# Four single B tiles loaded in two or three parts each, and fifteen one-word loads by SyncE

## The chip, the cores and the metric

One core of one Trainium2 chip. The metric is device microseconds of one execution, as the median of several runs. All runs quoted here are fast.

## The reference

```python
def setup_inputs():
    B, N = 8, 2176
    return {"a": randn(B, N, N) as float32, "b": randn(B, N, N) as float32}

def reference(a, b):
    prod = np.matmul(a, b)
    return np.diagonal(prod, axis1=1, axis2=2).sum(axis=-1)      # 8 numbers
```

The trace of a product needs no product: it is the sum over all i, j of a[i, j] * b[j, i]. The kernel has to read 303 MB and to do one multiply and add for each pair of elements.

## The kernel before

For each of the eight products it loads A in two double tiles (128 partitions x 2 x 4 rows) and one single tile (128 x 1 row), transposes A on TensorE, loads B in tiles of the same kinds, and multiplies and sums on VectorE. GpSimd issues nearly all loads, in one fixed order, and each casts float32 to bfloat16 on its way. The buffers are three deep.

```python
stage = ctx.enter_context(tc.tile_pool(name="stage", bufs=3))
single = ctx.enter_context(tc.tile_pool(name="single", bufs=3))
# ... (cut)
loaded = []

def in_order():
    return tc.issue_after(loaded[-1].ins) if loaded else nullcontext()

def load(src, start, m, count):
    if m == 1:
        t = single.tile([P, 1, N], bf16, tag="single")
    else:
        t = stage.tile([P, DOUBLE * ROWS, N], bf16, tag="stage")
    rows = src[start:start + P * m * count, :].rearrange("(g p r) k -> p g r k", g=count, r=m)
    part = t[:, 0:count * m, :].rearrange("p (g r) k -> p g r k", r=m)
    with in_order():
        issued = nc.gpsimd.dma_start(out=part, in_=rows)
    loaded.append(issued)
    groups = [(start + g * P * m, m, t[:, g * m:(g + 1) * m, :]) for g in range(count)]
    return groups, issued
# ... (cut: transposes of A, evacuation, products)
for start, m, count in ([(*g, 1) for g in b_groups] if last else joined(b_groups)):
    # ... (cut: the last tile of the last product)
    groups, _ = load(b[bi], start, m, count)
    for start, m, b_t in groups:
        # ... (cut: the multiply-and-sum on VectorE)
# ... (cut: sums over the partitions by TensorE)
nc.sync.dma_start(out=out.rearrange("(a b) -> a b", a=1), in_=tiles["result"][:1, :BATCH])
```

SyncE does two things only: the first tile of A, and the eight results at the end.

## Time and profile before

| | before |
|---|---|
| median, runs | 710.44 us (710.42 to 710.47, 2 runs) |
| span of the profiled run | 708.7 us |
| last load landed | 705.28 us |
| output issued, landed | 706.78, 707.87 us |
| packets of GpSimd's queue q0 | 11,472 |
| packets of SyncE's queue q1 | 146 |

How to read it: all times within a run count from the start of its span. A load is cut into packets for sixteen DMA engines. In a single tile a packet is one row, 4,352 bytes as written; in the double tiles it is four rows, 17,408 bytes. "Row" below means one of 4,352 bytes. Each engine finishes its share by itself and then adds one to the load's semaphore, so the trace has sixteen completion times for one load of GpSimd, and the load has landed with the last of them. I call the engine that completes last the latest engine, and the distance from the first completion to the last one the spread. The records name no engine, so the sixteen times are only a sorted list. The lines of the profile that carry the reading stand in the prediction below.

```profile
SPq L342 <- DMA out_dram<-result: 0.4, 1, 0.4
```

### The profile page before, as it was taken

The numbers are of one execution on the slowest core, as the hardware profiler recorded it, in microseconds if no ns is written. First come the engines' busy times: TensorE is split into PE (matmuls) and PEld (weight loads), VectorE is DVE, ScalarE is ACT, GpSimd is POOL, SyncE is SP. The second block draws the span as 40 slices with busy tenths as digits, with TensorE's granted clock in tenths as the row PEclk, the third lists the DMA queues.
The fourth block names the chain that finished last, engine by engine and source line by source line (L and its number), as shares of the span: only waits on it lengthen the run. The fifth ranks groups of instructions, "written<-read, shape, count | busy, mean of one in ns | idle before, by whom it ended". The sixth has DMA issues, their size and how long they took to land.

```text
span 708.7 us, 3573 instructions
## 1 busy us (share of the span) xinstructions
PE 197.8 (28%) x1342; PEld 184.2 (26%) x1342; DVE 420.6 (59%) x455; ACT 196.8 (28%) x210; POOL 35.0 (5%) x61
## 2 busy tenths in 40 slices
PE   1542006420055100551006600056000670006705
PEld 0542005410054100550006500056000560005605
DVE  0223996139952399523994349943499334993396
ACT  2344005430064200652006510066000670006700
POOL 1000000000010000100001000000000000000010
PEclk9977556765577655776557765577655775557765
DMA  9999999999999999999999999999999999999997
GB/s 220 220 220 214 209 221 220 219 210 213 223 219 213 214 218 220 219 211 214 220 220 216 212 216 220 217 214 214 220 220 215 213 217 219 217 216 214 217 215 143
DMA packets 11635, 152.30 MB, mean 215 GB/s; under 512 B 866, under 2 KB 1122, under 8 KB 3298
## 3 DMA queue, kind: packets, MB, share of 16 engines
q0 software_dynamic: 11472, 150.97, 100.1%
q1 hardware_dynamic: 146, 1.11, 0.4%
q8 instruction: 10, 0.16, 0.1%
q14 instruction: 7, 0.06, 0.0%
HBM read 303.04 MB, written 0.00 MB: 428 GB/s over the span
## 4 chain that ended last, share of the span: by engine, by line
DMA 54%; DVE 29%; another core or an unknown queue 10%; PE 3%; issue 2%; ACT 1%; POOL 1%; DVEq 0%; POOLq 0%
DMA t<-in_b_dram 42%; DVE scratch L132 29%; DMA t<-in_a_dram 12%; PE ps L165 2%; ACT at L122 1%; POOL t L83 1%; PE trace_ps L293 0%; DVE acc L132 0%; DVEq L132 0%; PE ps L186 0%; POOL identity masks.py:199 0%; DVE at L120 0%; PE total L308 0%; POOL identity masks.py:197 0%
## 5 line engine op out<-in xcount | busy, mean ns | idle before, releaser
L132 DVE CUSTOM_DVE_ANT_1 scratch<-at,t 128x2048 bf16<-128x2048 bf16 (+1 forms) x159 | 319.6, 2010 | 76.7 <-DMA t<-in_b_dram 69.4
L122 ACT COPY at<-ps 128x1024 bf16<-128x1024 bf16 x208 | 194.5, 1039 | 472.0 <-PE ps L165 472.0
L165 PE MATMUL ps<-identity,t 128*128 128x128 f32 x1071 | 176.8, 332 | 480.5 <-DMA t<-in_a_dram 255.4
L165 PEld LDWEIGHTS ps<-identity,t 128*128 128x128 f32 x1071 | 164.9, 213 | 489.2 <-DVE sums L285 322.0
L120 DVE COPY at<-ps 128x1024 bf16<-128x1024 bf16 (+2 forms) x104 | 93.6, 903 | 201.0 <-PE ps L165 183.7
L83 POOL DMA_DIRECT2D t<-in_a_dram x23 | 15.4, 669 | 357.8 <-DVE acc L132 213.3
L83 POOL DMA_DIRECT2D t<-in_b_dram x27 | 17.0, 632 | 292.8 <-DVE acc L132 145.0
L186 PE MATMUL ps<-identity,t 128*128 128x128 bf16 x170 | 16.4, 219 | 5.3 <-DVE at L120 5.0
L293 PE MATMUL trace_ps<-t,at 128*128 128x128 bf16 x80 | 9.6, 290 | 22.7 <-DMA t<-in_b_dram 22.3
L293 PEld LDWEIGHTS <-at 128*128 128x128 bf16 x89 | 9.8, 122 | 23.6 <-issue 22.9
L186 PEld LDWEIGHTS <-t 128*128 128x128 bf16 x170 | 13.0, 100 | 8.5 <-issue 8.3
L132 DVE DVE_READ_ACCUMULATOR2_ANT acc<- 128x1 f32 x166 | 13.6, 82 | 0.0
L96 DVE CAST t<-words 128x1088 bf16<-128x1088 f32 x1 | 0.7, 727 | 5.0 <-DMA words<-in_a_dram 5.0
L132 DVE CUSTOM_DVE_ANT_1 scratch<-at,b_t 128x256 bf16<-128x256 bf16 (+1 forms) x3 | 1.5, 515 | 1.6 <-DMA b_t<-in_b_dram 1.6
L132 DVE CUSTOM_DVE_ANT_0 scratch<-at,t 128x128 bf16<-128x128 bf16 x7 | 2.0, 291 | 0.2
L95 ACT CAST t<-words 128x1088 bf16<-128x1088 f32 x1 | 1.1, 1098 | 3.8 <-DMA words<-in_a_dram 3.8
L258 POOL DMA_DIRECT2D b_t<-in_b_dram x3 | 1.6, 567 | 0.0
L285 DVE TENSOR_REDUCE sums<-acc 128x1 f32<-128x22 f32 (+1 forms) x8 | 1.4, 174 | 0.3
L95 ACT ACT_TABLE_LOAD x1 | 1.3, 1283 | 0.7 <-PEq L331 0.7
L293 PE MATMUL trace_ps<-b_t,at 128*128 128x128 bf16 x9 | 1.3, 290 | 0.0
L308 PE MATMUL total<-late,ones 128*1 128x1 f32 x8 | 0.5, 163 | 0.3 <-DVE late L132 0.3
masks.py:199 POOL TENSOR_SCALAR_AFFINE_SELECT identity<-identity 128x128 f32<-128x128 f32 (+1 forms) x2 | 0.5, 307 | 0.0
(14 smaller groups left out, 2.4 us busy)
## 6 DMA issues: line engine op xcount, KB each, us to landing
t<-in_a_dram POOLq DMA_DIRECT2D x16, 4352.0 KB, 44.1
t<-in_b_dram POOLq DMA_DIRECT2D x14, 4352.0 KB, 51.8
t<-in_b_dram POOLq DMA_DIRECT2D x3, 2176.0 KB, 32.4
t<-in_b_dram POOLq DMA_DIRECT2D x9, 544.0 KB, 54.8
t<-in_a_dram POOLq DMA_DIRECT2D x7, 544.0 KB, 45.5
words<-in_a_dram SPq DMA_DIRECT2D x1, 1088.0 KB, 5.1
t<-in_b_dram POOLq DMA_DIRECT2D x1, 1088.0 KB, 14.7
b_t<-in_b_dram POOLq DMA_DIRECT2D x1, 256.0 KB, 19.6
```

The lines of the kernel that those rows point to most:

```text
L83: issued = nc.gpsimd.dma_start(out=part, in_=rows)
L95: nc.scalar.copy(out=t[:, 0, :half], in_=plain[:, :half])
L96: nc.vector.tensor_copy(out=t[:, 0, half:], in_=plain[:, half:])
L120: last_copy = nc.vector.tensor_copy(out=dst, in_=src)
L122: nc.scalar.copy(out=dst, in_=src)
L132: nc.vector.tensor_tensor_reduce(out=out, in0=x, in1=y, scale=1.0, scalar=0.0, op0=MUL, op1=ADD, accum_out=acc,)
L165: nc.tensor.transpose(ps[:, n * m + r, :], words[:, r, c0:c0 + step * (P - 1) + 1:step], tiles[f32],)
L186: last_transpose = nc.tensor.transpose(ps16[:, n, r, :], a_t[:, r, c0:c0 + P], tiles[bf16],)
L258: loaded.append(nc.gpsimd.dma_start(out=row[:, lo:hi], in_=b[bi, start:start + P, lo:hi]))
L285: nc.vector.reduce_sum(out=tiles["sums"][:, bi:bi + 1], in_=acc[:, :cols], axis=mybir.AxisListType.X)
L293: nc.tensor.matmul(trace_ps, x, y, start=(n == 0), stop=(n == len(pe_work) - 1),)
L308: nc.tensor.matmul(total[:, BATCH - 1:BATCH], tiles["ones"], part, start=(n == 0), stop=(n == len(parts) - 1),)
```

## The change

The single B tile of products 1 to 4 (the products count from 0) is loaded in parts of unequal partition counts. SyncE also loads single words to 1, 2, ... 15 partitions, once the third load has landed; nothing reads them. The bytes of A and B stay the same. The intent is to see how a load whose partition count is no multiple of sixteen is dealt to the sixteen DMA engines.

```diff
+    SPLIT_SINGLES = {
+        1: ((0, 120), (120, P)),
+        2: ((0, 120), (120, 124), (124, P)),
+        3: ((0, 104), (104, 116), (116, P)),
+        4: ((0, 112), (112, P)),
+    }
+    MARKS = 15
...
+            parts = SPLIT_SINGLES.get(bi, ((0, P),)) if m == 1 else ((0, P),)
...
-        with in_order():
-            issued = nc.gpsimd.dma_start(out=part, in_=rows)
-        loaded.append(issued)
+        for lo, hi in parts:
+            with in_order():
+                if len(parts) == 1:
+                    issued = nc.gpsimd.dma_start(out=part, in_=rows)
+                else:
+                    issued = nc.gpsimd.dma_start(out=part[lo:hi], in_=rows[lo:hi])
+            loaded.append(issued)
...
+        if bi == 0:
+            marks = const.tile([MARKS, MARKS], f32, tag="marks")
+            for n in range(1, MARKS + 1):
+                begun = nc.sync.dma_start(out=marks[0:n, n - 1:n], in_=a[0, 0:n, 0:1])
+                tc.add_manual_dep(begun.ins, loaded[2].ins.name, ...)   # after the third load
```

More of the change, by code (lines that the diff above doesn't have):

```diff
@@ L72, in in_order, with load @@
         return tc.issue_after(loaded[-1].ins) if loaded else nullcontext()
-    def load(src, start, m, count):
+    def load(src, start, m, count, parts=((0, P),)):
         if m == 1:
@@ L270 @@
                 continue
-            groups, _ = load(b[bi], start, m, count)
+            parts = SPLIT_SINGLES.get(bi, ((0, P),)) if m == 1 else ((0, P),)
+            groups, _ = load(b[bi], start, m, count, parts)
             for start, m, b_t in groups:
@@ L283 @@
                     on_dve(at[:, v0:v0 + m, split:], b_t[:, 0:m, split:])
+        if bi == 0:
+            marks = const.tile([MARKS, MARKS], f32, tag="marks")
+            for n in range(1, MARKS + 1):
+                begun = nc.sync.dma_start(out=marks[0:n, n - 1:n], in_=a[0, 0:n, 0:1])
+                tc.add_manual_dep(
+                    begun.ins, loaded[2].ins.name,
+                    mybir.DependencyInfo(
+                        mybir.DependencyClass.Sync, mybir.DependencyReason.DATA
+                    ),
+                    reason="after the third load",
+                )
         nc.vector.reduce_sum(
```

## The prediction

> **What bounds the kernel now.** I read the page first: the busy shares, the slices and the table of DMA queues.
>
> ```profile
> PE 197.8 (28%) x1342; PEld 184.2 (26%) x1342; DVE 420.6 (59%) x455; ACT 196.8 (28%) x210; POOL 35.0 (5%) x61
> ...
> DMA  9999999999999999999999999999999999999997
> ...
> q0 software_dynamic: 11472, 150.97, 100.1%
> q1 hardware_dynamic: 146, 1.11, 0.4%
> q8 instruction: 10, 0.16, 0.1%
> q14 instruction: 7, 0.06, 0.0%
> HBM read 303.04 MB, written 0.00 MB: 428 GB/s over the span
> ```
>
> No compute engine is over 59% busy, while the sixteen DMA engines are busy in every slice but the last, and the queue that GpSimd feeds accounts for 100.1% of their time. The time is the DMA work of the busiest DMA engine, plus a short tail. The packet count of q0 can be rebuilt from the program: 30 double loads of 256 rows, 3 of 128, 17 loads of one or two rows a partition of 128 and 3 partial ones of 128 make 10,624 row packets, and 53 loads with 16 completion packets each make 848; the sum is 11,472. So one row is one packet, and every load ends with sixteen completions.
>
> Next the issues with their time to landing, and the order in time of GpSimd, to see how deep the queue is.
>
> ```profile
> t<-in_b_dram POOLq DMA_DIRECT2D x14, 4352.0 KB, 51.8
> ...
> t<-in_b_dram POOLq DMA_DIRECT2D x9, 544.0 KB, 54.8
> ```
> ```profile
> 109.72 0.70 POOL L83 DMA_DIRECT2D t<-in_b_dram x1 [19.24 <-DVE acc L132]
> 123.78 1.27 POOL L83 DMA_DIRECT2D t<-in_b_dram x2 [13.37 <-PE ps L186]
> 145.70 0.70 POOL L83 DMA_DIRECT2D t<-in_a_dram x1 [20.65 <-PE ps L186]
> ```
>
> A double load of 4352 KB needs 4.456 MB / 215 GB/s = 20.7 us of the sixteen engines, and it lands 43 to 61 us after its issue. There is always more than one whole double load ahead of a new one: the queue is at least 20 us deep. The issue gaps of 13 to 21 us on GpSimd therefore cost nothing, and a few issues more there do not either.
>
> Last the end of the span in half microseconds (the last two columns are the DMA share and GB/s).
>
> ```profile
> 702.00:702.50 0.50, 0.00 (x0) 0.00 (x0) 0.47 (x3) 0.00 (x0) 0.00 (x0) 1.00 1.01 172
> 702.50:703.00 0.50, 0.40 (x4) 0.40 (x4) 0.14 (x1) 0.00 (x0) 0.00 (x0) 1.00 0.80 138
> 703.00:703.50 0.50, 0.50 (x6) 0.50 (x5) 0.00 (x0) 0.00 (x0) 0.00 (x0) 1.00 0.66 114
> 703.50:704.00 0.50, 0.50 (x7) 0.50 (x6) 0.20 (x1) 0.00 (x0) 0.00 (x0) 1.00 0.32 52
> 704.00:704.50 0.50, 0.50 (x7) 0.50 (x5) 0.49 (x2) 0.00 (x0) 0.00 (x0) 1.00 0.22 38
> 704.50:705.00 0.50, 0.50 (x8) 0.50 (x6) 0.43 (x2) 0.00 (x0) 0.00 (x0) 0.67 0.10 15
> ```
>
> These lines are a taper, not a cliff: the engines finish one after another over almost 3 us. The trace's completion events say the same: the sixteen completions of the last load come between 2.82 us before the last one and the last one at 705.28 us; sorted, the latest three are at 0, -0.20 and -0.40 us, the next at -1.20. The first load's sixteen spread over only 0.50 us. What pulled them apart stands in the packet records: ten instruction fetches of 16 KB, 0.89 to 1.03 us each, and seven of 8 KB during the run, 0.32 us each, land on single engines, and after the one at 51.57 us one engine's completions stay 0.9 us behind the others. An engine that falls behind never catches up, because its queue is never empty. That is the fact on which this prediction rests.
>
> **What the Trainium skill says.** "DMA: Bandwidth & Descriptors", section "Where 436 GB/s comes from", gives 435 GB/s as the ceiling of sixteen engines; the 428 GB/s read here lies 2% under it, so each engine runs near its own limit and work moved to one engine cannot be done faster there. The same page, section "Why a DMA increments its semaphore by 16 and not by 1", says that a load is split over the largest k up to 16 that divides the partition counts; that on the GpSimd path all sixteen engines post a completion whatever k is; that k below 16 takes k consecutive engines from a round-robin cursor; that loads from SyncE take the lowest-numbered k; and, as an exception on this chip, that some direct copies on the GpSimd path use k = 16 with the partitions divided by 16 and rounded up. Every load before has 128 partitions, so only the sixteen completions are confirmed (848 = 53 x 16); no record of before shows any other k. Section "Queues, rings and completion order" says that an engine with work on two queues switches between them at packets; the instruction fetches agree: the one at 108.09 us took 0.32 us and put one engine about 0.3 us back, with no further loss to the switch.
>
> **The change part by part.** Nothing is computed differently; the order of each compute engine stays, GpSimd has 59 loads in place of 53, SyncE 15 more.
>
> Row cost: 4,352 B packets took 0.342 us each; single loads, eight rows an engine, land 2.57 to 2.66 us after the load ahead of them, so 0.325 us a row. I use that.
>
> Bytes and rows of the four tiles: the same 4 x 128 rows; moved to other engines only.
>
> Distribution, with the skill's divisors: 120 goes on 15 engines with 8 rows, 104 on 13 with 8, 112 on 16 with 7, 16 on 16 with 1, and 8, 4, 4, 12, 12 on as many engines with 1 row each. With the cursor at c before the first of them, 120 skips engine c+15; 8 goes to c+15 and c to c+6; 120 then starts at c+7 and skips c+6, the fours take c+6 to c+13; 104 takes c+14 to c+10 and skips three, the twelves take c+11 to c+6 and c+7 to c+2. Against 32 rows an engine for four whole tiles, three engines end with +3, eight with +2, five with -5 (9 + 16 - 25 = 0). The largest surplus costs 3 x 0.325 = 0.98 us, +2 costs 0.65 us.
>
> What that does to the end depends on where the surplus meets the lag. The latest engine of before has +2 or +3 with a chance of 11 in 16; if it has -5, the next one, 0.2 us ahead of it, most likely has. The last completion therefore moves by about +0.5 to +1.0 us, mean +0.75.
>
> Completions: 6 loads more, one packet of 22 ns on each engine: 6 x 0.022 = 0.13 us, on every engine.
>
> SyncE's fifteen loads: 120 words and, if the lowest k engines complete, 120 completions: the first engine has 15 + 15 packets, the sixteenth none. The completions of the SyncE queue took 9 ns before; with that for all 30, 0.27 us on the first engine, 0.14 on a middle one. They start after the third load, which landed at 68.4 us, with SyncE otherwise idle to the end; nothing reads them.
>
> GpSimd: 6 issues more of 0.53 to 0.70 us, about 4 us in all, each next to a gap of 13 to 21 us: 0. DVE waits for two or three completions in place of one, in a stage where it waits for DMA anyway: 0.
>
> The semaphores: loads rotate over eight, and the sixth to eighth load of a batch now waits for the one eight earlier. Eight loads earlier is a batch earlier, some 87 us, and a load lands within 61 us at most: 0.
>
> Sum: 0.75 + 0.13 + 0.1 = about 1.0 us. 710.44 + 1.0 = 711.4 us. All of it lies on the path that sets the end, as lateness of the latest DMA engine.
>
> **The rivals.**
> 1. The k = 16 exception, always from the first engine: 120 leaves the last engine empty, 104 gives 7 rows to 14 engines and 6 to one. Then four engines have +4, four +2, four +1 and the last -24. At most +1.3 us, but three chances in four that the latest engine has +2 or less; with marks on the same low engines 710.7 to 712.1. The profile can't tell it from the cursor.
> 2. Each row goes to the engine that serves its partition in a whole tile: no imbalance, only completions and words: 710.7. Against it: the skill's rule for the small loads.
> 3. Only powers of two as k: 120 and 104 on 8 engines with 15 and 13 rows. If these were the same eight engines each time, they would get +7+1, +7+2 and +5+6 rows (each twelve on four engines, three rows each), 28 x 0.325 = 9.1 us: 719.5. Still 1.3%, within 2%.
> 4. A single engine for a whole part. A single 120-row part would put 112 rows too many on it: 36 us, 747. It is the only way to be slower by over 2% that I see; the counts chosen all have divisors, so the rule speaks against it.
> 5. A small load stalls its engine for a whole round trip to memory. Fifteen of these on the first engine with some 0.3 us each would be 4 to 5 us: 715. The fetches that interleave without loss speak against it.
> 6. It hides: the latest engine happens to be spared each time, or the larger program moves instruction fetches to other engines. A fetch of 16 KB is worth 1 us, so this alone is a lottery of -0.5 to +1 us, and I widen the range for it. Faster by 2% is impossible while all 151 MB still have to come at this rate.
>
> **The range.** The sum with surplus from +0.3 to +1.3 us, marks to +0.3 and the fetches' lottery gives 710.5 to 712.8 us for 8 times in 10. Within 2% (under 724.6) holds rivals 1, 2, 3, 5 and 6: 0.97. Slower by over 2% is rival 4 or a stall unseen so far: 0.025. Faster: 0.005.
>
> **What would show it.** Queue q0 should have 59 x 16 + 10,624 = 11,568 packets, with the same bytes; q1 should have 146 + 240 = 386 if each of fifteen loads posts k completions (or 506 if sixteen). The taper at the end should be longer than 2.8 us, since five engines have 5 rows, 1.6 us, less to do; were the row placement of rival 2 true, it would stay at 2.8. The spread of a load's sixteen completions should widen right after each of the first three split tiles and not after the fourth. A DMA share well under 0.9 in a slice near 70 us, or a double load that lands more than 22 us after the one ahead, would show a stall and make the prediction wrong; so would a step of 2 us or more in the landing of one split tile.

## More of the kernel before

```profile
L342 SPq EVENT_SEMAPHORE  x8: 17/28/28, 707.2 to 708.7; - x8
L342 SPq DRAIN  x3: 7/7/7, 707.9 to 708.3; - x3
```

The first is from SyncE's waits (total us, times, longest), the other from the instructions of the closing line (durations in ns, first and last start). SyncE passes its closing waits one by one; the output's is the last of them that takes time, and 0.08 us after the output landed SyncE is through, at 707.95 us.

## The result, and the profile after

712.13 us (712.07 to 712.20, 2 runs) against 710.44: +1.69 us. A ratio in this document is the mean time of one kernel's fast runs over that of the other's of the same rounds, so it is not quite the ratio of the medians: here 1.0023, interval 1.0002 to 1.0043. That is inside the predicted range of 710.5 to 712.8 and within 2%. The predicted rise was 1.0 us, the measured one 1.7. All outputs are right.

The queues of the changed kernel:

```profile
q0 software_dynamic: 11632, 150.97, 100.0%
q1 hardware_dynamic: 386, 1.12, 0.5%
q8 instruction: 10, 0.16, 0.1%
q14 instruction: 7, 0.06, 0.0%
HBM read 303.04 MB, written 0.00 MB: 427 GB/s over the span
```

The bytes are those of before and the engines are as full. But q0 has 11,632 packets, and the prediction said 11,568: there are 64 more than its rule for the split allows.

The end of the span in half microseconds (busy times of PE, PEld, DVE, ACT and POOL with their counts, PE clock, DMA share, GB/s), to lay beside the taper of before:

```profile
703.00:703.50 0.50, 0.00 (x0) 0.00 (x0) 0.50 (x1) 0.00 (x0) 0.00 (x0) 0.50 0.92 154
703.50:704.00 0.50, 0.11 (x2) 0.11 (x2) 0.34 (x3) 0.00 (x0) 0.00 (x0) 0.50 0.82 142
704.00:704.50 0.50, 0.50 (x6) 0.50 (x5) 0.00 (x0) 0.00 (x0) 0.00 (x0) 0.50 0.42 71
704.50:705.00 0.50, 0.50 (x7) 0.50 (x5) 0.00 (x0) 0.00 (x0) 0.00 (x0) 0.50 0.06 10
705.00:705.50 0.50, 0.50 (x7) 0.50 (x6) 0.40 (x1) 0.00 (x0) 0.00 (x0) 0.50 0.08 13
705.50:706.00 0.50, 0.50 (x7) 0.50 (x6) 0.45 (x3) 0.00 (x0) 0.00 (x0) 0.50 0.07 13
706.00:706.50 0.50, 0.50 (x7) 0.50 (x5) 0.29 (x2) 0.00 (x0) 0.00 (x0) 0.50 0.03 5
```

From 704.5 to 706 us the share is 0.06 to 0.08, which is one engine in sixteen (0.0625): for the last 1.7 us a single engine works while fifteen have nothing left. In the kernel before three engines shared the last microsecond. The completion times of some loads, sorted (I took them from the trace's semaphore events; this is no view of the profiler), show how that came about:

```
completions relative to the load's last one, us (earliest, second, ..., third latest, second latest)
                                        earliest  second      third   second latest   last at
before, 8-row load ahead of tile 1        -1.70    -1.48  ...  -0.87     -0.20         176.66
after,  8-row load ahead of tile 1        -1.47    -1.25  ...  -0.50     -0.00         176.53
after,  tile 1, last part (120+8)         -3.37    -1.25  ...  -0.30     -0.03         179.28
after,  tile 2, last part (120+4+4)       -6.31    -1.59  ...  -0.41     -0.02         267.28
after,  tile 3, last part (104+12+12)     -9.53    -2.53  ...  -0.44     -0.42         355.45
after,  tile 4, last part (112+16)        -9.97    -2.67  ...  -0.52     -0.52         442.93
after,  last load                         -6.77    -3.36  ...  -1.73     -1.70         706.53
before, last load                         -2.82    -2.61  ...  -0.40     -0.20         705.28
```

One engine, always only one, gets 1.9 to 2.6 us further ahead of the second one at each of the first three tiles and no more than 0.3 at the fourth; eight rows of 0.32 us would be 2.6. From the third tile on it completes ten to eleven microseconds before the latest engine, for over 300 us, until the loads of the last product are issued too late for it: at 672.11 us it has finished all that was issued, and the next load is issued at 672.47. So in each of the parts of 120 and 104 partitions, one and the same engine had nothing to do.

The other end of the list shows who sets the end. Over tile 2 the last completion falls back against the mean of the sixteen by 0.68 us (1.19 us on the double load ahead of the tile, 1.87 on the next one), which is two rows, and over tile 3 by 0.32 us (1.81 to 2.13), one row; the kernel before has +0.04 and -0.05 there. Two more rows at tile 2 fit the engines that get a row of both fours. Over tile 4 there are another 0.48 us, but not from its parts: an instruction fetch of 8 KB is recorded at 454.16 us, and run 11, in which this tile is whole, has 0.54 us there.

Then the end. SyncE's waits and closing instructions after, beside those shown of before:

```profile
SPq L302 <- DMA t<-in_b_dram: 67.3, 1, 67.3
SPq L302 <- DMA marks<-in_a_dram: 15.1, 7, 2.6
SPq L368 <- DMA out_dram<-result: 0.7, 1, 0.7
```
```profile
L368 SPq EVENT_SEMAPHORE  x11: 17/28/28, 708.3 to 710.4; - x11
L368 SPq DRAIN  x3: 7/7/7, 709.6 to 709.9; - x3
```

The output landed at 709.08 us, 1.22 us later than before; SyncE was through at 709.59, which is 1.64 us later. It has three closing instructions more, and the order of the waits changed. The seventeenth load of SyncE, the output, uses the first of its eight semaphores again; the seven others now come after it in the row. The trace has these waits 0.06 us apart (709.10, 709.16, 709.22, ... 709.53 us), so the seven cost 0.43 us in the open, although their loads had landed 600 us earlier.

So of the 1.7 us of span, 1.25 are a later last load, and 0.43 are these waits. The two explain all of it; the rest of the tail is as before (last load to output issue 1.50 us in both).

### The profile page after: what moved, and what is told of

Same layout as the page of the kernel before. It is cut to its first block, busy times and chain, and to the rows that moved or that the text cites. A ratio compares the mean times of both kernels' runs of the same rounds, so it can differ in the third digit from the quotient of the medians.

```text
span 710.4 us, 3600 instructions
## 1 busy us (share of the span) xinstructions
PE 197.8 (28%) x1342; PEld 184.4 (26%) x1342; DVE 420.6 (59%) x455; ACT 196.8 (28%) x210; POOL 38.4 (5%) x67
## 3 DMA queue, kind: packets, MB, share of 16 engines
q0 software_dynamic: 11632, 150.97, 100.0%
## 4 chain that ended last, share of the span: by engine, by line
DMA 54%; DVE 35%; another core or an unknown queue 4%; PE 3%; issue 2%; POOL 0%; DVEq 0%; POOLq 0%
DMA t<-in_b_dram 42%; DVE scratch L144 34%; DMA t<-in_a_dram 12%; PE ps L177 2%; DVE at L132 1%; PE trace_ps L319 0%; DVE acc L144 0%; POOL t L93 0%; PE ps L198 0%; DVEq L144 0%; POOL identity masks.py:199 0%; POOL identity masks.py:197 0%; PE total L334 0%; DVE result L338 0%
## 5 line engine op out<-in xcount | busy, mean ns | idle before, releaser
L93 POOL DMA_DIRECT2D t<-in_b_dram x23 | 14.8, 643 | 294.0 <-PE ps L198 145.4
L95 POOL DMA_DIRECT2D t<-in_b_dram x10 | 5.4, 545 | 0.0
```

What stands on the lines that cost most here:

```text
L95: issued = nc.gpsimd.dma_start(out=part[lo:hi], in_=rows[lo:hi])
```

## The experiments

Theory A at the start: loads of GpSimd are dealt from the first engine in shares of the partitions divided by sixteen and rounded up, and an uneven deal costs what the latest engine gets too much; the words cost nothing but the closing waits. Rivals: the number of loads costs; the words delay the engines; a cursor moves small loads round the engines.

All runs were against the kernel before on the same chip, five rounds each (of the run with eight parts four runs were fast). "Last load" is from the profiled run, against 705.28 of before, which was profiled only once; "open" is the time from the output's landing to SyncE's end of waits.

| run | median us | against before | last load us | open us |
|---|---|---|---|---|
| changed kernel again | 712.04 | +1.59 | 706.28 | 0.51 |
| words only | 710.79 | +0.34 | 705.21 | 0.51 |
| splits only | 711.32 | +0.87 | 706.05 | 0.08 |
| splits, 14 word loads | 711.61 | +1.16 | 706.34 | 0.08 |
| even splits | 710.53 | +0.14 | 705.25 | 0.08 |
| 120+4+4 in seven tiles | 715.01 | +4.62 | 709.51 | 0.08 |
| 127+1 in seven tiles | 710.74 | +0.35 | 705.48 | 0.08 |
| eight parts of 16 in seven tiles | 726.72 | +16.33 | 720.08 | 0.08 (then GpSimd's closing, run 8) |
| 46 word loads of 15 | 710.88 | +0.46 | 705.64 | 0.08 |
| 46 word loads of 4 | 710.48 | +0.06 | 705.28 | 0.08 |
| 112+12+4 in one tile | 710.38 | -0.04 | 705.30 | 0.08 |
| 112+12+4 in two tiles | 710.70 | +0.28 | 705.38 | 0.08 |

The median of the kernel before was 710.45, 710.39 and 710.42 in the three groups (the first four rows, the next four, the last four), with single runs from 710.18 to 710.82. The intervals of the ratios are some 0.13% to each side, 0.9 us. Differences under half a microsecond are thus read from the profile's times, and the medians only agree with them.

### 1. The changed kernel again

No edit.

> The changed kernel unaltered, to have it beside its parts on one chip. It should repeat 712.1 us (711.9 to 712.3), 1.7 us over the kernel before, with the last load landing about 1.25 us later than in the kernel before and the stretch from the landing of the output to the end about 0.43 us longer.

712.04 us (711.75 to 712.18), ratio 1.0021, interval 1.0007 to 1.0035. It repeats. But its last load landed at 706.28, not 706.53: the same kernel differs by 0.25 us from profile to profile in this number, and smaller differences of it between kernels prove nothing alone.

### 2. Words only

```diff
-    SPLIT_SINGLES = {1: ..., 2: ..., 3: ..., 4: ...}
+    SPLIT_SINGLES = {}
```

> Only SyncE's fifteen word loads; the tiles are whole again. Theory A (the words cost nothing on the DMA engines to speak of, but their seven further completion semaphores are waited for one after another at the end, 0.06 us each, after the output has landed): +0.5 us, 710.8 to 711.1, with the last load landing no more than 0.15 us later than before. Rival (the words delay the DMA engines, the end is free): the landing of the last load moves by the whole difference. Rival (all of the 1.7 us comes from the split): 710.4 to 710.5.

710.79 us, +0.34, at the lower edge of the theory's range. The last load is 0.07 us earlier than before, the open stretch 0.43 longer: 0.36 us, all of it closing waits. The rival that the words delay the engines falls here.

### 3. Splits only

```diff
-        if bi == 0:
+        if False:
             marks = const.tile([MARKS, MARKS], f32, tag="marks")
```

> Only the four split tiles, no word loads. Theory A (uneven rows on the DMA engines, +4 rows on the first four engines, 1.3 us at most): +1.2 us, 711.5 to 711.8, last load landing about 1.2 us later than before, the end as before, q0 11,632 packets. Rival (the words are what delays): 710.5 to 710.8.

+0.87 us; the last load 0.77 later, under the 1.2 that I expected from the profile of the changed kernel. The packets are the 11,632 expected, and the closing is that of before. Alone the parts add up to 0.87 + 0.34 = 1.21 us, and together they make 1.59. That 0.4 is dealt with after run 4.

### 4. Splits and fourteen word loads

```diff
-    MARKS = 15
+    MARKS = 14
```

> The changed kernel with fourteen word loads in place of fifteen. The output's load then uses the last of the eight semaphores of SyncE instead of the first. Theory A: the seven waits at the end are passed while the output is still on its way, so that the 0.43 us vanish: 711.6 to 711.8, though seven of eight semaphores are in use still and 105 of 120 words are loaded. Rival (the 0.43 us are the price of the number of word loads or semaphores): 712.0 to 712.1.

711.61 us, against 712.04 for fifteen: the 0.43 us are gone, with one word load less. The last loads are at 706.34 and 706.28, so nothing else changed. The waits for the output:

```profile
SPq L368 <- DMA out_dram<-result: 0.3, 1, 0.3
```

The output is now the sixteenth load of SyncE and has the last semaphore; the other seven waits are passed while it is on its way. It is the place of the output's semaphore in the row that costs, not the number of word loads.

Against the splits alone there is still +0.29 us in time and in the last load. The single runs hardly overlap (711.49 to 711.73 against 711.29 to 711.53), so this is probably no chance: words cost something beside splits. Run 9 below makes some 0.1 us of that plausible for the words themselves. What the rest is no run shows; in the last load alone it lies within the 0.25 us by which one kernel's profiles differ.

### 5. Even splits

```diff
-        1: ((0, 120), (120, P)),
-        2: ((0, 120), (120, 124), (124, P)),
-        3: ((0, 104), (104, 116), (116, P)),
+        1: ((0, 64), (64, P)),
+        2: ((0, 64), (64, 96), (96, P)),
+        3: ((0, 96), (96, 112), (112, P)),
         4: ((0, 112), (112, P)),
```
(and no word loads)

> The same four tiles in the same numbers of loads (2, 3, 3, 2), but cut at multiples of sixteen partitions (64+64; 64+32+32; 96+16+16; 112+16), no word loads. Theory A (only the unevenness costs; a load more costs one completion of 22 ns on each engine): +0.13 us, 710.5 to 710.7; q0 10,624 + 944 = 11,568 packets without filling; the sixteen completions of a load spread at the end as in the kernel before, 2.8 us. Rival (it is the number of loads that costs, 0.2 us each): 711.6.

710.53 us, the last load at 705.25, the spread at the end 2.48 us.

```profile
q0 software_dynamic: 11568, 150.97, 100.2%
```

Six loads more by GpSimd cost nothing that can be told from zero here (+0.14 us in time, -0.03 in the last load), so it is the unevenness. And with parts that are multiples of sixteen, q0 has exactly 10,624 + 59 x 16 packets: the 64 extra ones come from the uneven parts. They can be counted: a part of p partitions has ceil(p/16) packets on each of sixteen engines, and where there is no row left the packet is a filling of 4 bytes (the queue has 1,008 packets of 4 bytes, 59 x 16 completions and 64). For 120, 8, 120, 4, 4, 104, 12 and 12 the fillings are 8 + 8 + 8 + 12 + 12 + 8 + 4 + 4 = 64. This is the deal of the prediction's first rival.

### 6. 120+4+4 in seven tiles

```diff
+    SPLIT_SINGLES = {n: ((0, 120), (120, 124), (124, P)) for n in range(7)}
```
(and no word loads)

> 120+4+4 in all seven single B tiles of the first seven products, no word loads. Theory A (every load is dealt from the first engine in shares of its partitions divided by 16 and rounded up, so that each pair of fours adds two rows to the first four engines): 14 rows x 0.325 = 4.5 us more on these: 714.3 to 715.2; q0 10,624 + 67 x 16 + 7 x 32 = 11,920 packets. Rival (a cursor moves the fours round the engines, 15 + 4 + 4 engines a tile): the surplus spreads, at most some 3 to 6 rows on one engine: 711.2 to 712.5.

715.01 us, ratio 1.0064, interval 1.0052 to 1.0077; the last load 4.22 us later. The packets and a part of the taper:

```profile
q0 software_dynamic: 11920, 150.97, 99.6%
```
```profile
705.50:706.00 0.50, 0.31 (x3) 0.15 (x2) 0.50 (x1) 0.00 (x0) 0.00 (x0) 0.50 0.26 48
706.00:706.50 0.50, 0.00 (x0) 0.00 (x0) 0.50 (x1) 0.00 (x0) 0.00 (x0) 0.50 0.28 50
706.50:707.00 0.50, 0.16 (x2) 0.16 (x2) 0.31 (x3) 0.00 (x0) 0.00 (x0) 0.50 0.28 48
```

A share of 0.26 to 0.28 is four engines of sixteen (0.25): the same four got both fours of every tile, fourteen rows too many, and they are what is left at the end. The last load's completions sorted have four at 0, -1.41, -1.52 and -2.24, and the next at -3.98. 11,920 is the number that the rounded-up deal gives. The cursor falls for loads of four rows: it would have spread them.

The run also says how far ahead these four were: fourteen rows of 0.325 us are 4.55 us, with fourteen completions of 0.022 us 4.86, and the end moved by 4.22. So the latest of the four lay some 0.3 to 0.6 us ahead of the latest engine of all (an estimate). The four rows of the changed kernel, 1.3 us, should then move the end by 0.8 to 1.0 us; run 3 measured 0.77.

### 7. 127+1 in seven tiles

```diff
+    SPLIT_SINGLES = {n: ((0, 127), (127, P)) for n in range(7)}
```
(and no word loads)

> 127+1 in the same seven tiles, no word loads. 127 is prime. Theory A (shares of eight rows from the first engine, seven on the last; the single row goes to the first engine): the first engine has +7 rows, 2.3 us, the last -7: 710.44 + 2.3 less what the first engine lay ahead of the latest one: 711.5 to 713.0. Rival (the largest divisor up to 16 of 127 is 1, all rows on one engine): 119 rows x 0.325 = 39 us a tile, well over 750 us. Rival (cursor for the single rows): 710.4 to 711.2.

710.74 us, the last load 0.20 us later. This is under the theory's 711.5, and the prime count did no harm either. The packets say why:

```profile
q0 software_dynamic: 11696, 150.97, 100.2%
```

10,624 + 60 x 16 = 11,584 would be all without fillings; 112 are left, 16 a tile. 127 takes one filling. The other fifteen are the single row, which went out as sixteen packets: the records have 112 packets of 272 bytes (4,352 / 16), and there are none in the other runs. A load of one partition is cut along its row, over all sixteen engines, and so it burdens none. I had expected the row to go to the first engine; one engine, with seven rows of 127, gained a row each time (it now completes the last load 4.3 us ahead of the latest engine, against 2.8 us in the kernel before), and the single rows cost nobody much. This agrees with the Trainium skill, "DMA: Bandwidth & Descriptors", section "Why a DMA increments its semaphore by 16 and not by 1": the number of engines goes by the slowest dimension whose size is not 1, and here that is the row's 2,176 elements, which 16 divides.

### 8. Eight parts of 16 in seven tiles

```diff
+    SPLIT_SINGLES = {n: tuple((c, c + 16) for c in range(0, P, 16)) for n in range(7)}
```
(and no word loads)

> Each of the seven single B tiles in eight loads of 16 partitions, no word loads: 49 loads more, perfectly even. Theory A: 49 completions x 22 ns = 1.1 us on every engine, 711.4 to 711.8, if the queue stays filled. But here the seventh and eighth part wait for the two double loads issued just before them, since there are only eight completion semaphores; GpSimd stands some 50 us and issues the next double load at the last moment. If the queue runs dry for some tenths of a microsecond in each of seven products, 713 to 716; the landings of the next double load would show it as a step over 21 us after the landing of the last part.

726.72 us, ratio 1.0231, interval 1.0217 to 1.0245: slower by three times what I allowed for. The deal is perfectly even (12,256 packets = 10,624 + 102 x 16). GpSimd in order of time, around the tile of the second product:

```profile
125.25 1.96 POOL L90 DMA_DIRECT2D t<-in_b_dram  x4
134.30 0.49 POOL L90 DMA_DIRECT2D t<-in_b_dram  x1 [7.08 <-DMA t<-in_a_dram]
136.94 0.48 POOL L90 DMA_DIRECT2D t<-in_b_dram  x1 [2.16 <-DMA t<-in_a_dram]
158.31 0.48 POOL L90 DMA_DIRECT2D t<-in_b_dram  x1 [20.88 <-DMA t<-in_b_dram]
179.03 0.48 POOL L90 DMA_DIRECT2D t<-in_b_dram  x1 [20.25 <-DMA t<-in_b_dram]
179.60 2.05 POOL L88 DMA_DIRECT2D t<-in_a_dram  x3
```

With eight completion semaphores a load waits for the landing of the one eight before it. The eighth part waits for the double load issued just ahead of the tile, and the next double load of A, which GpSimd issued at 145.7 us in the kernel before, is issued at 179.6, when the queue is down to the last part. The last part lands at 181.57 us and the double behind it at 203.16, 21.6 us after it in place of 20.5: the queue ran dry for 1.1 us. In all seven products this step is 21.6 to 22.2 us, where the kernel before has 20.5 to 21.1. And the spread of the completions is 1.31 us at the seventh part and 0.27 at the eighth: all engines stood idle and started level again.

I read that as a cost that I had not thought of. While the queue stays full, a fetch of instructions holds up one engine here and another there, and only the final sum for the latest engine counts. A queue that runs dry makes everyone wait for the latest engine each time. Per product that is 1.1 us dry plus about 1.0 us for the latest engine (at the seventh part the second latest is 0.85 us ahead of it), in seven products about 15 us; the last load is 14.8 us later. This sum is an estimate from these rows, not separately tested.

The other 1.5 us are at the end: GpSimd's own closing wait (its DRAIN) ended 4.21 us after the last load, in place of 2.21 us before and 2.46 us in the changed kernel. With 102, 53 and 59 loads (and 2.78 us with the 67 of run 6) this is 0.04 us a load; in the runs with up to 60 loads it hides behind SyncE's end.

### 9 and 10. Forty-six word loads

```diff
-    MARKS = 15
+    MARKS = 46
-                begun = nc.sync.dma_start(out=marks[0:n, n - 1:n], in_=a[0, 0:n, 0:1])
+                begun = nc.sync.dma_start(out=marks[0:15, n - 1:n], in_=a[0, 0:15, 0:1])   # second run: 0:4
```
(and no splits)

> No split tile; 46 word loads of 15 partitions each by SyncE (46, so that the output again has the last of the eight semaphores and nothing is added at the end). Theory B (each word and each completion takes its 22 ns from the engine, on the lowest-numbered fifteen engines): 46 x 2 x 0.022 = 2.0 us later on all but the sixteenth, so the last load lands about 2.0 us later and the time is 712.3 to 712.6. Rival (words slip between the row packets at no cost): 710.4 to 710.6.

> As the run before, with 4 partitions a load. Theory B: only the first four engines are later by 2.0 us. From the fours in seven tiles I work out that the latest of these four lay some 0.6 us ahead of the latest engine of all in the kernel before, so that the last load lands 1.2 to 1.5 us later: 711.7 to 712.0. Rival (the four words go to engines other than the first four, or cost nothing): 710.4 to 710.9.

Both expectations failed. With 15 partitions: 710.88 us, the last load 0.36 us later, not 2.0. With 4: 710.48, the last load where it was. The packets are all there:

```profile
q1 hardware_dynamic: 1526, 1.12, 0.7%
```

1,526 = 146 + 46 x (15 + 15), nearly all shown with 22 ns; with 4 partitions there are 514 = 146 + 46 x (4 + 4). So k engines post k completions, as the Trainium skill, "DMA: Bandwidth & Descriptors", section "Why a DMA increments its semaphore by 16 and not by 1", says of SyncE's loads. The 22 ns of a record are not what a word takes from the engine: 0.36 us / 46 = 8 ns for a word and its completion together. Even with the scatter of 0.25 us and the 0.20 us by which the second latest engine lay ahead it is under 18 ns, not 44. Records overlap and must not be added up: a row's record is 0.342 us long, and a row costs 0.325. For fifteen or fourteen loads 8 ns make 0.1 us. The second run can't show a cost on the first four engines of less than the 0.3 to 0.6 us by which they lay ahead (run 6).

### 11 and 12. A try to gain by an uneven split

```diff
+    SPLIT_SINGLES = {1: ((0, 112), (112, 124), (124, P))}       # second run: in products 1 and 3
```
(and no word loads)

> A try at a kernel faster than both: one tile cut 112+12+4, so that engines 12 to 15 get seven rows of it in place of eight and engines 0 to 3 nine. If the three latest engines of the kernel before are among 12 to 14 (the split kernel, which relieved these, no longer had them as the latest) and the latest of the first four lies 0.6 us ahead, the last load lands 0.2 to 0.3 us earlier: 710.1 to 710.3 against 710.4. If they are elsewhere: 710.45 to 710.8.

> The same in two tiles: engines 12 to 15 have two rows less, engines 0 to 3 two more, which now should be the latest: 0.6 us ahead less 0.65 us makes +0.05, with completions +0.1: 710.4 to 710.6, no better than before and worse than one tile by 0.2 to 0.3. If the one tile didn't help because the latest engines are elsewhere: 0.65 us worse, 711.0 to 711.2.

710.38 and 710.70 us; the last load at 705.30 and 705.38. Each time lies between the two ranges that I had expected. One tile gained nothing, two lost a little. After one, two of the three latest engines are 0.49 and 0.57 us earlier than the last one at 705.30, where they had been 0.20 and 0.40 earlier than 705.28: so two were probably relieved, and the one that sets the end wasn't. It may be one of the first four (nine rows now), or one of 4 to 11, whose share did not change. The records name no engine, and with a scatter of 0.25 us the time does not decide. No version that I ran beats the kernel before; what there is to win is the distance of the latest engine from the mean, which is 1.6 us by the last load's sixteen completions, 0.2%.

## Why the prediction was right or wrong

**The bound: right.** DMA is at 100% of sixteen engines in both, the bytes are the same, and a late engine stays late. The run with 120+4+4 shows it on four engines over 600 us, the leading engine of the changed kernel over 300 us. The comparison of 428 with 435 GB/s isn't needed for that, and it is loose: the section "Where 436 GB/s comes from" works the 435 out for the sixteen ports into SBUF, which took 215 GB/s here, while the 428 were read from HBM. Right with one limit that the prediction gave in passing: it holds while the queue is never empty. Run 8 emptied it.

**The distribution: wrong in its rule.** The step that failed is "Distribution, with the skill's divisors", 15 engines for 120 and 13 for 104 with a cursor for the rest. The measured packets (64 fillings), the one engine that leads by three times eight rows, and the four engines of run 6 are the deal that the prediction listed as its first rival: sixteen shares, rounded up, always beginning at the same engine (that it is the lowest-numbered one, the records do not show). By that deal four engines have +4 rows, not three +3, and one has -24, not five -5. That the size came out near is luck: the prediction's mean of 0.75 us came from two or three rows on the latest engine, and the 0.77 us of the splits alone (with words 1.0 to 1.25) from four rows on engines that had lain 0.3 to 0.6 us ahead of it. The first rival had allowed up to 1.3.

**Completions and issues: right, within what can be seen.** 0.13 us predicted, +0.14 in time and -0.03 in the last load for six more even loads.

**The words: the term was mis-sized twice.** 0.1 us was put in for them, as time on the engines. It is 0 to 0.1 there when the tiles are whole; beside the splits 0.29 us are left, mostly unexplained (run 4). But "nothing reads them" left out that the program's end waits for every semaphore in use: 0.43 us in the open, shown by run 4, where it vanished with one load less. This term is most of what is missing from 1.0 us to the measured 1.7.

**The semaphores: right for the change.** No load of the changed kernel waits for the one eight before it: in the split tiles that one had landed 33 us or more ahead of the issue. Run 8, with five parts more in a tile, does, and pays 14.8 us.

**The lottery of fetches:** the range was widened for it by -0.5 to +1 us. That much was not seen: two profiles of one kernel differ by 0.25 us, and no run traces this to a fetch. But a fetch can cost more than its record: the one at 627.92 us has 0.32 us, and in the kernel before the latest engine falls back by 0.47 us against the mean at that time (0.83 to 1.30).

**The signs that were named.** q1 386 packets: right. q0 11,568: wrong, 11,632. A taper longer than 2.8 us: right, 6.77 us, but by one engine and not five. A spread that widens after three tiles and not after the fourth: right, but for the 0.5 us of the fetch near the fourth. No step of 2 us in a landing and no stall near 70 us: right.

## What to carry to other kernels

When DMA bounds a kernel with a full queue, the end is set by the DMA engine that is furthest behind, so cut tiles at multiples of sixteen partitions; each row too many on that engine (4,352 bytes written here) costs 0.32 us, and nothing gives it back while the queue stays full. Look at how many loads are under way beside the number of completion semaphores: more small parts than that stop the issuing engine and can empty the queue, which cost 14.8 us here, over three times the worst uneven split. And count the end of the program: semaphores that are waited for after the output has landed cost 0.06 us each, and the place of the output among them decides whether they do.

## What the Trainium skill lacked or had wrong

- "DMA: Bandwidth & Descriptors", section "Why a DMA increments its semaphore by 16 and not by 1": it gives the divisor with a cursor as the rule for loads of GpSimd and the rounded-up shares as an exception for "some direct copies". Here every load of GpSimd with 4 to 127 partitions whose count is no multiple of 16 was dealt the second way, and all of them cast: 64 fillings in the changed kernel, 11,920 packets in run 6, one engine left out by 120 and 104.
- The same section does not say that engines without a row get filling packets: 64 of them, and 8 for each part of 120.
- No page that I read has the closing waits of a program: 0.06 us for each semaphore that SyncE waits for after the output has landed, and a closing of GpSimd that grows by 0.04 us a load (2.21 us with 53 loads, 4.21 us with 102).
- "Runtime: NRT & Kernel Launch", section "Instruction fetch mechanics", calls the cost of crossing a 16 KiB boundary of instructions mostly hidden. Whether it is for the engine that runs the instructions was not looked at; in a kernel bound by DMA it is not for the DMA engine that carries the fetch: 0.89 to 1.03 us in its record, and after the one at 51.57 us one engine's completions 0.9 us behind the others.
- No page that I read says what a 4-byte packet costs an engine that has rows queued. Its record of 22 ns is not that: 46 loads of 15 words moved the end by 0.36 us and not by 2.0.
